# A decoder layer on one core: the matmuls that turn the 1/rms of queries and keys come later in the program, and one output-gate pair moves ahead of the convolutions

## The chip, the core and the metric

The kernel runs on one core of a Trainium2 chip. The metric is device time in microseconds (us), lower is better. Before the change three runs took 2025.02, 2026.25 and 2028.8 us, with a median of 2026.25 us.

## The reference, cut to what matters

One layer of a hybrid decoder, SEQ = 1024 tokens of D_MODEL = 1024, float32 throughout:

```python
x = x + 0.5*(1+gate0) * swiglu1(rmsnorm(x)*(1+scale0)+shift0)
u = (rmsnorm(x)*(1+scale1)+shift1) @ w_in       # in-projection
x = x + (1+gate1) * concat(diff_attention(...), mlstm(...)) @ w_out
x = x + 0.5*(1+gate2) * swiglu2(rmsnorm(x)*(1+scale2)+shift2)

# differential attention: 4 heads, two 64-wide queries and keys each
q = rmsnorm(q.reshape(..., 4, 2, 64), g_q); k = rmsnorm(k.reshape(..., 4, 2, 64), g_k)
q = partial_rope(q, cos, sin);              k = partial_rope(k, cos, sin)
# mLSTM: q and k go through a causal convolution of 4 taps and silu;
# its result h is gated:  sigmoid(o_pre) * h
```

The change touches the in-projection alone: the rms of queries and keys, the values and the output gate of the mLSTM, and the convolutions.

## The kernel before, in words

The layer runs in stages one behind the other: the first feed-forward block to about 715 us, the in-projection to about 1085, the heads (attention and mLSTM, interleaved) to about 1276, the out-projection to about 1390, the second feed-forward block to the end.

**A product.** The in-projection is made of calls of `wino` (L240), each giving a 256x1024 piece of u, transposed, by a Winograd scheme on halves: seven products of 512x128 by 512x512, each of 12 matmuls, since every operand is split into a high and a low part and three of the four cross products are kept (`mm3`, L199 to L201). In a call the products come in the order B11, T2, T1, B21, T3, B22, T4. Their weights come by DMA on SyncE's queue (`wraw`), are summed (`wsum`, L194, `sf`), rounded by ScalarE (`split_w`, L187, `whi`) and subtracted by VectorE (L188, `wlo`). VectorE combines the products into the four quarters of the result (L229): "11" is what B11 and B21 add up to and is handed out by `got11`, "22" and "12" come after T3 and B22, "21" after T4.

**The calls around the change.** Four calls `wqk[0..3]` give queries (0, 1) and keys (2, 3), then `wmv[1]` gives the second half of the mLSTM's values, `wcv[0..3]` what the four convolutions need, and `wmo[0]`, `wmo[1]` the output gates. Then the heads begin.

**The rms of queries and keys.** Each quarter of a query or key is squared by ScalarE and added up by VectorE (`k`, L582 to L587). When both calls of the queries are through, `qk_finish` (L591) is put into the list `pending`, which the next `wino` runs behind its product T1 (`late`). It sums the squares over each 64 rows by eight small matmuls (L598; the profile shows two records for each such float32 matmul), takes the reciprocal root on VectorE by ten short instructions (L601, then `rsqrt`, L349 to L354), and for each half of the tokens copies the result sixteenfold (ScalarE, L605, tile `c`), turns it by four matmuls against the identity (L609) and copies it out of PSUM (ScalarE, L611). `qk_turned` (L614) multiplies queries or keys by it, applies the rotary part, rounds (L628, `qhi`), takes the rest (L629) and writes both to memory (`qkd`, L631) on SyncE's queue.

**Values, convolutions and gates.** A quarter of the values is turned by four transposes (L642, into `modps`), copied by ScalarE (L644, `vt`) and stored. These turns too wait in `pending` for the next call. `got11` of a convolution copies its quarter into `cu` (ScalarE, L746); L735 to L739 are the taps, silu and the store to `mlqk`, 512 KB each. `got11` of an output gate is a tanh (ScalarE, L756, tile `vc`) followed by a multiply and a store to `mlo`, 256 KB each. The tiles `cu` lie where the tiles `qraw` of queries and keys lay (`pq.close()` gives up the one pool and the next takes its space).

**What sets the order.** The program's text is not the order: a scheduler that simulates a time line sets the order of instructions on each engine, subject to dependencies and priorities (`split_w` has a raised one). `keep_in_program_order` holds an instruction behind the one traced before it on its engine. Each engine then runs its own list strictly in that order.

Of the kernel before, what the change touches and what calls it, by code (L numbers as in the profile page):

```python
# [25 lines left out]
P = 128  # L26
# [107 lines left out]
class Layer:  # L134
    def __init__(self, tc, A, es):
        self.tc, self.nc, self.A, self.es = tc, tc.nc, A, es
        nc = self.nc
        pool = lambda name, **k: es.enter_context(tc.tile_pool(name=name, **k))
        self.const = pool("const", bufs=1)
        c = self.const  # L140
        self.ones = c.tile([P, 1], F32, name="ones")
        nc.vector.memset(self.ones, 1.0)
        self.eps = c.tile([P, 1], F32, name="eps")
        nc.vector.memset(self.eps, EPS)
        self.mod = c.tile([P, 72], F32, name="mod")
        self.G = c.tile([P, 24], F32, name="G")
        self.gate = c.tile([P, 24], F32, name="gate")
        self.bada = c.tile([P, 72], F32, name="bada")
        self.gn = c.tile([P, 24], F32, name="gn")
        self.cs = c.tile([P, KT], F32, name="cs")  # L150
        self.B, self.full = {}, {}
        self.nct = 3
        self.sums = nc.gpsimd
        self.pending = []

    def ps(self):
        return self.mmps.tile([P, HT], F32, tag="mm", name="mm")
# [4 lines left out]
    def late(self):  # L162

        p, self.pending = self.pending, []
        for f in p:
            f()

# [58 lines left out]
    def wino(self, src, got11, out, got, st=None):  # L226

        nc = self.nc
        add = lambda o, a, b: nc.vector.tensor_tensor(out=o, in0=a, in1=b, op=ALU.add)  # L229
        t = lambda n: self.tmp.tile([P, HT], F32, tag=n, name=n)  # L230
        r1, r2 = self.load_raw(src[0]), self.load_raw(src[1])
        a11, a21, a12, a22 = r1[:, 0], r1[:, 1], r2[:, 0], r2[:, 1]
        if st is None:
            x = self.ps()
            self.prod(x, self.split_w(a11), "B11", True)
            p1 = t("p1")
            nc.scalar.copy(out=p1, in_=x)
            s1 = self.wsum(a21, a22, ALU.add)
            s2 = self.wsum(s1, a11, ALU.subtract)
            y6, z5 = self.ps(), self.ps()  # L240
            self.prod(y6, self.split_w(s2), "T2", True)
            u2 = t("u2")
            add(u2, p1, y6)
            self.prod(z5, self.split_w(s1), "T1", True)
            self.late()
            w = t("w")
            add(w, u2, z5)
            self.prod(x, self.split_w(a12), "B21", False)
            got11(x)
            y7, z3 = self.ps(), self.ps()  # L250
            self.prod(y7, self.split_w(self.wsum(a11, a21, ALU.subtract)), "T3", True)
            c22 = out("22")
            add(c22, w, y7)
            self.prod(z3, self.split_w(self.wsum(a12, s2, ALU.subtract)), "B22", True)
        else:
            p1 = st["p1"]
            s1 = self.wsum(a21, a22, ALU.add)
            s2 = self.wsum(s1, a11, ALU.subtract)
            z3, z5, y7, y6 = (self.ps() for _ in range(4))
            self.prod(z3, self.split_w(self.wsum(a12, s2, ALU.subtract)), "B22", True)  # L260
            self.prod(z5, self.split_w(s1), "T1", True)
            self.late()
            self.prod(y7, self.split_w(self.wsum(a11, a21, ALU.subtract)), "T3", True)
            self.prod(y6, self.split_w(s2), "T2", True)
            u2 = t("u2")
            add(u2, p1, y6)
            w = t("w")
            add(w, u2, z5)
            c22 = out("22")
            add(c22, w, y7)  # L270
        got("22", c22)
        c12 = out("12")
        add(c12, w, z3)
        got("12", c12)
        self.prod(y7, self.split_w(a22), "T4", False)
        c21 = out("21")
        add(c21, u2, y7)
        got("21", c21)
# [312 lines left out]
    def qk_finish(self, which):  # L591

        nc = self.nc
        ps = self.ps()
        for hf in range(2):
            for i in range(4):
                c = 8 * (4 * hf + i)
                nc.tensor.matmul(ps[:, c:c + 8], self.accs[which][hf][:, i * P:(i + 1) * P], self.bd[:, 0:P:16],  # L598
                                 start=True, stop=True, skip_group_check=True)
        v, y, t = (self.qkp.tile([P, 64], F32, tag=f"qn{i}", name=f"qn{i}") for i in range(3))  # L600
        nc.vector.tensor_scalar(out=v, in0=ps[:, 0:64], scalar1=1.0 / 64, scalar2=EPS, op0=ALU.mult, op1=ALU.add)  # L601
        self.rsqrt(y, t, v)
        for hf in range(2):
            r = self.ct()
            nc.scalar.copy(out=r.rearrange("p (c d) -> p c d", d=16),  # L605
                           in_=y[:, 32 * hf:32 * hf + 32].unsqueeze(2).broadcast_to([P, 32, 16]))
            ps = self.ps()
            for i in range(4):
                nc.tensor.matmul(ps[:, i * P:(i + 1) * P], r[:, i * P:(i + 1) * P], self.ident,  # L609
                                 start=True, stop=True, skip_group_check=True)  # L610
            nc.scalar.copy(out=r, in_=ps)  # L611
            self.qk_turned(which, hf, r)

    def qk_turned(self, which, hf, r):  # L614
        nc = self.nc
# [359 lines left out]
def build(tc, yT, **A):  # L975
    nc = tc.nc
    with ExitStack() as es:
        L = Layer(tc, A, es)
# [40 lines left out]
        rs = []  # L1019
# [122 lines left out]
        def mlv_store(pr):  # L1142
            def store(e, hf, v):
                nc.sync.dma_start(out=L.mlv[2 * pr + e][:, 4 * hf:4 * hf + 4, :], in_=v)
            return store
# [37 lines left out]
        L.rst = load_const(L.gp, "rst", [P, T])  # L1183
        L.wino(A["wdv"][0], *dvh[0], starts[0])
        late, L.pending = L.pending, []
        L.gate_rows(graw)
        turn, L.pending = L.pending, late
# [23 lines left out]
        for which in range(2):  # L1211
            for tp in range(2):
                i = 2 * which + tp
                seen, out, got = L.qk_handlers(which, tp)
# [8 lines left out]
                    L.wino(A["wqk"][i], seen11, out, got)  # L1223
            L.pending.append(lambda w=which: L.qk_finish(w))
        L.wino(A["wmv"][1], *L.v_handlers(mlv_store(1)))
        pq.close()

        pq, qpool = stack("right")
        L.cvp = qpool("cvp", bufs=2)
        for h in range(4):  # L1230
            L.wino(A["wcv"][h], *L.conv_handlers(h))
        for pr in range(2):
            L.wino(A["wmo"][pr], *L.o_handlers(pr))
        pq.close()
        pm.close()
        pt.close()
# [132 lines left out]
```

## Time and profile before

| | |
|---|---|
| median of three runs | 2026.25 us (2025.02 to 2028.8) |
| profiled execution | 2028.85 us, its span 2027.1 us |
| mean granted clock of TensorE | 0.976 of full speed |
| TensorE busy | 1924.4 us, 95% of the span |
| VectorE, ScalarE, GpSimd busy | 73%, 38%, 14% |
| TensorE's longest waits, 860 to 1110 us | 9.7 (L883), 9.1 in four (L609), 3.4 (L642) |

PE is TensorE, ACT ScalarE, DVE VectorE, POOL GpSimd and SP SyncE. An idle time stands in brackets behind an instruction, with what released it. PEclk is the clock granted to TensorE as a share of 2.4 GHz; 0.50 is its lower level, 1.2 GHz, and a value between is a stretch in which it changed. Times are us from the start of the span.

### The profile page before, as it was taken

To read this page: it belongs to the slowest core of one execution; us is meant where nothing else is said; L and a number is where in the kernel's file an instruction comes from. 1 tells how busy PE (TensorE), PEld (TensorE's weight loads), DVE (VectorE), ACT (ScalarE), POOL (GpSimd) and SP (SyncE) were. 2 spreads that over 40 slices of the span, in tenths; PEclk is the share of its full clock that TensorE was granted. 3 is DMA by queue.
4 is the path that set the end of the run, shared out by engine and by line. 5 is a ranking of instruction groups with operands and counts; after the bars stand their busy time and mean duration, and the time that the engine had idled before them with its cause. 6 is when DMAs were issued, how large, how long until landed. Compare 5 with 4: busy or idle time off the path is not lost.

```text
span 2027.1 us, 24590 instructions
## 1 busy us (share of the span) xinstructions
PE 1924.4 (95%) x8870; PEld 1588.1 (78%) x8870; DVE 1476.6 (73%) x2609; ACT 774.1 (38%) x1494; POOL 292.3 (14%) x249
## 2 busy tenths in 40 slices
PE   4999999999999988989997999988999999999999
PEld 3778888888888876777786877876888888888887
DVE  8998888777766679577794987479766555556665
ACT  4522232222232356334443876255222233222232
POOL 0111212211121100000002211004212111121120
PEclk9999999999999989988998999999999999999999
DMA  8344333223221242223427963121111111111113
GB/s 303 125 146 140 115 118 106 85 82 104 101 72 58 94 146 71 79 97 129 150 111 203 185 131 120 53 83 63 63 63 42 63 63 42 49 56 53 53 63 125
DMA packets 86794, 202.82 MB, mean 100 GB/s; under 512 B 10128, under 2 KB 18704, under 8 KB 86672
## 3 DMA queue, kind: packets, MB, share of 16 engines
q1 hardware_dynamic: 77504, 184.93, 26.6%
q0 software_dynamic: 7840, 14.75, 4.1%
q8 instruction: 70, 1.15, 0.2%
q10 hardware_dynamic: 1328, 1.57, 0.2%
q14 instruction: 52, 0.43, 0.1%
HBM read 174.02 MB, written 27.26 MB: 99 GB/s over the span
## 4 chain that ended last, share of the span: by engine, by line
PE 83%; DVE 8%; ACT 4%; DMA 3%; issue 1%; POOL 1%; SPq 0%; DVEq 0%; ACTq 0%; POOLq 0%
PE mm L199 25%; PE mm L200 25%; PE mm L201 25%; PE t L820 1%; DVE adaacc L324 1%; DVE S L378 1%; DVE wlo L188 1%; DMA qkd<-qhi 1%; PE s L793 1%; ACT S L380 1%; POOL sf L194 1%; DVE S L429 1%; DMA adac<-in_wada 1%; PE s L794 1%; PE t L816 0%
## 5 line engine op out<-in xcount | busy, mean ns | idle before, releaser
L187 ACT CAST whi<-wraw 128x512 fp32r<-128x512 f32 x308 | 190.9, 621 | 481.8 <-PE mm L200 454.6
L199 PE MATMUL mm<-S,whi 128*128 128x512 f32 x900 | 354.5, 395 | 7.4 <-ACT whi L187 3.1
L200 PE MATMUL mm<-S,whi 128*128 128x512 f32 x900 | 353.7, 393 | 0.0
L201 PE MATMUL mm<-S,wlo 128*128 128x512 f32 x900 | 352.8, 393 | 0.0
L529 DVE SCALAR_TENSOR_TENSOR x<-mm,gate,x 128x512 f32<-128x512 f32 x368 | 269.5, 745 | 95.1 <-PE mm L201 93.9
L187 ACT CAST whi<-sf 128x512 fp32r<-128x512 f32 x224 | 138.8, 621 | 414.9 <-PE mm L200 387.3
L188 DVE TENSOR_TENSOR wlo<-wraw,whi 128x512 fp32r<-128x512 f32 x300 | 210.4, 702 | 89.5 <-ACT whi L187 77.5
L200 PE MATMUL mm<-glo,whi 128*128 128x512 f32 x672 | 262.5, 391 | 0.0
L201 PE MATMUL mm<-ghi,wlo 128*128 128x512 f32 x672 | 261.6, 392 | 0.0
L199 PE MATMUL mm<-ghi,whi 128*128 128x512 f32 x672 | 260.8, 393 | 0.1
L194 POOL TENSOR_TENSOR sf<-wraw 128x512 f32<-128x512 f32 x84 | 120.9, 1439 | 597.4 <-DMA wraw<-in_w 380.6
L199 PEld LDWEIGHTS mm<-S,whi 128*128 128x128 f32 x900 | 171.2, 190 | 44.2 <-ACT whi L187 3.5
L201 PEld LDWEIGHTS mm<-S,wlo 128*128 128x128 f32 x900 | 170.8, 190 | 36.5 <-DVE wlo L188 0.8
L200 PEld LDWEIGHTS mm<-S,whi 128*128 128x128 f32 x900 | 170.9, 190 | 35.3
L188 DVE TENSOR_TENSOR wlo<-sf,whi 128x512 fp32r<-128x512 f32 x224 | 156.1, 697 | 38.4 <-ACT whi L187 38.0
L199 PEld LDWEIGHTS mm<-ghi,whi 128*128 128x128 f32 x672 | 126.8, 189 | 26.4 <-ACT ghi L522 0.6
L200 PEld LDWEIGHTS mm<-glo,whi 128*128 128x128 f32 x672 | 126.9, 189 | 26.2
L201 PEld LDWEIGHTS mm<-ghi,wlo 128*128 128x128 f32 x672 | 126.8, 189 | 26.3
L229 DVE TENSOR_TENSOR c<-w,mm 128x512 f32<-128x512 f32 x84 | 57.2, 686 | 99.5 <-PE mm L201 99.4
L194 POOL TENSOR_TENSOR sf<-wraw,sf 128x512 f32<-128x512 f32 x42 | 64.1, 1526 | 444.8 <-DVE wlo L188 356.0
L324 DVE SCALAR_TENSOR_TENSOR adaacc<-adac,cs,adaacc 128x256 f32<-128x256 f32 x196 | 110.0, 561 | 10.7 <-DMA adac<-in_wada 9.3
L199 PE MATMUL mm<-B11h,whi 128*128 128x512 f32 x248 | 99.6, 409 | 11.4 <-ACT B11h L383 7.2
(332 smaller groups left out, 3418.1 us busy)
## 6 DMA issues: line engine op xcount, KB each, us to landing
wraw<-in_w SPq DMA_DIRECT2D x142, 512.0 KB
adac<-in_wada SPq DMA_DIRECT2D x112, 256.0 KB
ok<-qkd POOLq DMA_DIRECT2D x32, 256.0 KB, 8.0
adaraw<-in_wada SPq DMA_DIRECT2D x12, 512.0 KB
wraw<-in_wo SPq DMA_DIRECT2D x12, 512.0 KB
x<-in_xT SPq DMA_DIRECT2D x16, 256.0 KB
xd<-x SPq DMA_DIRECT2D x16, 256.0 KB
wraw<-in_wqk SPq DMA_DIRECT2D x8, 512.0 KB
```

The source lines that it names most:

```text
L187: nc.scalar.copy(out=hi, in_=raw)
L188: (eng or nc.vector).tensor_tensor(out=lo, in0=raw, in1=hi.bitcast(F32), op=ALU.subtract)
L194: self.sums.tensor_tensor(out=s, in0=a, in1=b, op=op)
L199: nc.tensor.matmul(ps, whi, xhi, start=first, stop=False, skip_group_check=True)
L200: nc.tensor.matmul(ps, whi, xlo, start=False, stop=False, skip_group_check=True)
L201: nc.tensor.matmul(ps, wlo, xhi, start=False, stop=last, skip_group_check=True)
L229: add = lambda o, a, b: nc.vector.tensor_tensor(out=o, in0=a, in1=b, op=ALU.add)
L324: nc.vector.scalar_tensor_tensor(out=acc, in0=raws[k], scalar=self.cs[:, k:k + 1], in1=acc, op0=ALU.mult, op1=ALU.add)
L378: eng.tensor_tensor(out=h, in0=x, in1=r, op=ALU.mult)
L380: self.nc.scalar.activation(out=h, in_=h, func=AF.Identity, scale=self.G[:, g:g + 1], bias=self.mod[:, s:s + 1])
L429: e.tensor_tensor(out=T[n][1], in0=v, in1=T[n][0].bitcast(F32), op=ALU.subtract)
L529: self.nc.vector.scalar_tensor_tensor(out=x, in0=ps, scalar=self.gate[:, g:g + 1], in1=x, op0=ALU.mult, op1=ALU.add)
```

## The change

`qk_finish` now makes both sixteenfold copies first and puts the rest (turn, copy out, `qk_turned`) into a second list, `next`. A new `later()` runs that list right behind the product B21 of the call. The turning matmuls are held in program order. In the sequence of calls `wmo[0]` now stands right behind `wmv[1]`, ahead of the change of pools and of the convolutions; `wmo[1]` stays behind them. Line numbers of the changed kernel are 6 or 7 higher up to its sums (L605), then 13 or 14.

```diff
     def late(self):
 
         p, self.pending = self.pending, []
         for f in p:
             f()
 
+    def later(self):
+
+        p, self.next = self.next, []
+        for f in p:
+            f()
...
             self.prod(x, self.split_w(a12), "B21", False)
+            self.later()
             got11(x)
...
+        rs = []
         for hf in range(2):
             r = self.ct()
             nc.scalar.copy(out=r.rearrange("p (c d) -> p c d", d=16),
                            in_=y[:, 32 * hf:32 * hf + 32].unsqueeze(2).broadcast_to([P, 32, 16]))
-            ps = self.ps()
-            for i in range(4):
-                nc.tensor.matmul(ps[:, i * P:(i + 1) * P], r[:, i * P:(i + 1) * P], self.ident,
-                                 start=True, stop=True, skip_group_check=True)
-            nc.scalar.copy(out=r, in_=ps)
-            self.qk_turned(which, hf, r)
+            rs.append(r)
+
+        def turn():
+            for hf, r in enumerate(rs):
+                ps = self.ps()
+                for i in range(4):
+                    self.tc.keep_in_program_order(
+                        nc.tensor.matmul(ps[:, i * P:(i + 1) * P], r[:, i * P:(i + 1) * P], self.ident,
+                                         start=True, stop=True, skip_group_check=True))
+                nc.scalar.copy(out=r, in_=ps)
+                self.qk_turned(which, hf, r)
+        self.next.append(turn)
...
         L.wino(A["wmv"][1], *L.v_handlers(mlv_store(1)))
+        L.wino(A["wmo"][0], *L.o_handlers(0))
         pq.close()
...
         for h in range(4):
             L.wino(A["wcv"][h], *L.conv_handlers(h))
-        for pr in range(2):
-            L.wino(A["wmo"][pr], *L.o_handlers(pr))
+        L.wino(A["wmo"][1], *L.o_handlers(1))
         pq.close()
```

**ScalarE at the turn of the queries.** `c` is the sixteenfold copy, `qn` the reciprocal root. Before:

```order
L605 COPY c_7729<-qn1_7716 128x512
L611 COPY c_7729<-mm_7731 128x512
L605 COPY c_7766<-qn1_7716 128x512
L611 COPY c_7766<-mm_7768 128x512
L187 CAST whi_7922<-sf_7918 128x512
```

and now:

```order
L613 COPY c_7729<-qn1_7716 128x512
L613 COPY c_7731<-qn1_7716 128x512
L624 COPY c_7729<-mm_7751 128x512
L624 COPY c_7731<-mm_7786 128x512
L193 CAST whi_7922<-sf_7918 128x512
```

Both copies now stand ahead of both copies out of PSUM. On TensorE nothing moved at this place: in either kernel the eight turning matmuls follow the eight of the sums directly, and the product B21 of the call stands ahead of the sums.

**TensorE at the sums of the keys.** `mm_8111` are the sums, `modps` the turn of a value quarter, `mm_8052` is product B21 of the call `wmv[1]`, `mm_7979` product T4 of the last call of the keys. Before:

```order
L199 MATMUL mm_8052<-B21h3_205,whi_8210 128x512
L200 MATMUL mm_8052<-B21l3_206,whi_8210 128x512
L201 MATMUL mm_8052<-B21h3_205,wlo_8211 128x512
L598 MATMUL mm_8111<-bd_7335,k_7823 128x8 x4
L598 MATMUL mm_8111<-bd_7335,k_7865 128x8 x4
L642 MATMUL modps_8359<-ident_225,vc_8226 128x128 x4
L609 MATMUL mm_8136<-ident_225,c_8134 128x128 x4
L609 MATMUL mm_8173<-ident_225,c_8171 128x128 x4
L199 MATMUL mm_8228<-S50_6634,whi_8232 128x512
```

and now:

```order
L205 MATMUL mm_7979<-S43_6733,whi_8027 128x512
L206 MATMUL mm_7979<-S33_6735,whi_8027 128x512
L207 MATMUL mm_7979<-S43_6733,wlo_8028 128x512
L656 MATMUL modps_8351<-ident_225,vc_8226 128x128 x4
L605 MATMUL mm_8111<-bd_7335,k_7823 128x8 x4
L605 MATMUL mm_8111<-bd_7335,k_7865 128x8 x4
L622 MATMUL mm_8156<-ident_225,c_8134 128x128 x4
L622 MATMUL mm_8191<-ident_225,c_8136 128x128 x4
L205 MATMUL mm_8228<-S50_6634,whi_8232 128x512
```

The value transposes moved from behind the sums to ahead of them, and T4 of the keys, between which and the sums 28 matmuls stood before, now stands right ahead of the transposes and the sums. T4 gives the last quarter of the keys, whose squares go into `k_7823` and `k_7865`.

**ScalarE in the call behind the values.** `vt` are value quarters out of `modps`, `cu` the first quarter of convolution 0, `vc_8401` that of output gate 0. A name ending in `_49` in brackets is a semaphore: of an engine, or of a DMA queue slot (DMAHW). Before:

```order
L644 COPY vt_8372<-modps_8367 128x512 [waits PE_49]
L187 CAST whi_8490<-wraw_8485 128x512 [waits DMAHW1_49,PE_49]
L746 COPY cu_8292<-mm_8300 128x512 [waits DMAHW3_49,DMAHW7_49,DVE_49,PE_49]
L644 COPY vt_8380<-modps_8375 128x512 [waits PE_49]
L187 CAST whi_8514<-sf_8510 128x512 [waits DVE_49,PE_49,Activation_49]
L187 CAST whi_8532<-sf_8508 128x512 [waits PE_49,Activation_49]
L735 ACTIVATE cv_8450<-cu_8292,convb_6794,convw_6792 128x1024 [waits DVE_49,DMAHW1_49,Activation_49,Pool_49]
```

and now:

```order
L658 COPY vt_8364<-modps_8359 128x512 [waits PE_49]
L642 CAST qhi_8215<-qraw_8022 128x512 [waits DMAHW1_49,DVE_49]
L193 CAST whi_8487<-wraw_8482 128x512 [waits PE_49]
L770 ACTIVATE vc_8401<-mm_8292 128x512 [waits PE_49]
L642 CAST qhi_8221<-qraw_7999 128x512 [waits DMAHW3_49,DVE_49]
L193 CAST whi_8511<-sf_8507 128x512 [waits DVE_49,PE_49]
L658 COPY vt_8372<-modps_8367 128x512 [waits DMAHW2_49,PE_49]
L193 CAST whi_8529<-sf_8505 128x512 [waits PE_49]
L770 ACTIVATE vc_8425<-vc_8425 128x512 [waits DVE_49]
L658 COPY vt_8380<-modps_8375 128x512 [waits DMAHW6_49,PE_49,Activation_49]
L770 ACTIVATE vc_8448<-vc_8448 128x512 [waits DVE_49]
```

Where the copy into `cu` stood, which waits for DMAs, there is now the tanh of the output gate, which waits for TensorE alone. The copy into `cu` stands one call later:

```order
L770 ACTIVATE vc_8469<-vc_8469 128x512 [waits DVE_49]
L193 CAST whi_8611<-wraw_8484 128x512 [waits PE_49,Activation_49]
L193 CAST whi_8644<-wraw_8639 128x512 [waits DMAHW3_49,PE_49,Activation_49]
L760 COPY cu_8478<-mm_8486 128x512 [waits DMAHW7_49,DMAHW0_49,PE_49]
L193 CAST whi_8668<-sf_8664 128x512 [waits DVE_49,PE_49,Activation_49]
```

The last copy `vt_8380` now has a wait on a DMA slot that it had not. GpSimd's list is the same in both kernels. The list of ScalarE has seven loads of an activation table before and after. In the heads, some 110 of about 1,070 rows of TensorE's list stand in other places.

## Rows read from the trace of the kernel before

**Rows 1.** The page, busy time of TensorE, its share of the span and instructions.

```profile
PE 1924.4 (95%) x8870; PEld 1588.1 (78%) x8870; DVE 1476.6 (73%) x2609; ACT 774.1 (38%) x1494; POOL 292.3 (14%) x249
```

**Rows 2.** TensorE's waits from 860 to 1110: line, releaser, us in all, times, longest.

```profile
PE mm L883 <- DMA mq<-mlqk: 9.7, 1, 9.7
PE mm L609 <- ACT c L605: 9.1, 4, 3.5
```

**Rows 3.** TensorE's timeline, queries: start, us, instruction, idle before and releaser.

```profile
889.73 1.95 PE L598 MATMUL mm<-bd,k 128*128 128x8 f32 x16 [0.76 <-DVE k L587]
895.21 2.08 PE L609 MATMUL mm<-ident,c 128*128 128x128 f32 x8 [3.53 <-ACT c L605]
898.53 2.08 PE L609 MATMUL mm<-ident,c 128*128 128x128 f32 x8 [1.25 <-ACT c L605]
900.27 0.77 PE L199 MATMUL mm<-S,whi 128*128 128x512 f32 x1
```

**Rows 4.** Busy time in windows, queries: us, engines, then granted clock (PEclk), DMA.

```profile
894.00:895.00 1.00, 0.00 (x0) 0.00 (x0) 0.45 (x2) 0.46 (x1) 0.00 (x0) 0.60 0.12 49
...
904.00:905.00 1.00, 1.00 (x5) 0.82 (x4) 1.00 (x3) 0.00 (x0) 0.00 (x0) 0.78 0.00 0
...
907.00:920.00 13.00, 13.00 (x59) 10.76 (x58) 9.59 (x17) 5.23 (x11) 0.00 (x0) 1.00 0.48 167
```

**Rows 5.** TensorE's timeline, keys.

```profile
941.12 1.85 PE L598 MATMUL mm<-bd,k 128*128 128x8 f32 x16
942.82 0.64 PE L642 MATMUL modps<-ident,vc 128*128 128x128 f32 x4
946.49 2.08 PE L609 MATMUL mm<-ident,c 128*128 128x128 f32 x8 [3.04 <-ACT c L605]
949.82 2.08 PE L609 MATMUL mm<-ident,c 128*128 128x128 f32 x8 [1.25 <-ACT c L605]
```

**Rows 6.** Busy time in windows, keys.

```profile
945.00:946.00 1.00, 0.00 (x0) 0.00 (x0) 0.69 (x4) 0.17 (x1) 0.00 (x0) 0.70 0.86 311
...
955.00:956.00 1.00, 1.00 (x4) 0.76 (x4) 1.00 (x3) 0.00 (x0) 0.00 (x0) 0.68 0.00 0
```

**Rows 7.** VectorE's timeline after the query turn, and a group of ScalarE's lines.

```profile
916.72 0.69 DVE L229 TENSOR_TENSOR qraw<-w,mm 128x512 f32<-128x512 f32 x1 [3.30 <-DMA qkd<-qraw]
...
923.21 0.69 DVE L587 TENSOR_TENSOR k<-k,c 128x512 f32<-128x512 f32 x1
...
L586 ACT ACTIVATE c<-qraw 128x512 f32<-128x512 f32 x12 | 7.4, 630 | 3.0 <-DVE qraw L229 2.9
```

**Rows 8.** The stop at 984: chain, ScalarE's timeline, TensorE's timeline, windows.

```profile
976.03 7.04 DMA qkd<-qraw
...
970.40 0.62 ACT L628 CAST qhi<-qraw 128x512 fp32r<-128x512 f32 x1 [4.19 <-DMA qkd<-qhi]
...
983.23 0.59 ACT L746 COPY cu<-mm 128x512 f32<-128x512 f32 x1 [8.87 <-DMA qkd<-qraw]
...
984.36 1.11 PE L642 MATMUL modps<-ident,vc 128*128 128x128 f32 x4 [3.37 <-ACT vt L644]
...
983.00:989.00 6.00, 4.64 (x13) 3.87 (x14) 3.99 (x6) 3.82 (x6) 0.33 (x4) 0.50 0.44 168
989.00:990.00 1.00, 1.00 (x4) 0.76 (x4) 1.00 (x2) 0.00 (x0) 0.00 (x0) 0.61 0.58 219
```

**Rows 9.** Opening of the heads: ScalarE's queue, TensorE, and the window 1085 to 1097.

```profile
1084.85 0.44 ACTq L863 DMA_DIRECT2D mq<-mlqk  x1
1088.72 0.59 ACTq L864 DMA_DIRECT2D mv<-mlv  x1
...
1094.67 2.04 PE L883 MATMUL mm<-mq,mk 128*128 128x128 f32 x8 [9.68 <-DMA mq<-mlqk]
...
1085.00:1097.00 12.00, 2.33 (x11) 2.36 (x12) 0.72 (x4) 2.50 (x6) 0.00 (x0) 0.66 1.12 370
```

**Rows 10.** TensorE's waits from 1106 to 1290, the longest row.

```profile
PE s L793 <- ACT e L799: 4.7, 7, 1.3
```

More of the change, by code (lines that the diff above doesn't have):

```diff
@@ L153, in __init__ @@
         self.sums = nc.gpsimd
-        self.pending = []
+        self.pending, self.next = [], []
     def ps(self):
```

## The prediction

> **What bounds the kernel now.** I read the busy shares first, then TensorE's waits, then its timeline at each wait, with the granted clock beside it. TensorE is busy 95% of the span [rows 1], so the end moves by what TensorE idles and by what it does at half rate, and by little else. In the stretch that the change touches, its waits are few and long: one of 9.7 us for the first head's queries, then four of 9.1 us together for the copies that the turn needs [rows 2], and one of 3.4 us for a copy `vt` [rows 8]. Each is followed by a stretch at 0.50 of the clock. That is the second price of a stop, and often the larger one.
>
> **Queries.** The reader is to see one stop in two pieces: 3.53 us from the sums' end to the first turn, then 2.08 us of turning, then 1.25 us more, because the second copy waits behind the copy out of PSUM [rows 3]. With both copies made first the 1.25 us goes: a pass of ScalarE over a tile of this size takes 0.63 us [rows 7], so the second copy ends that much behind the first, and the first half's turn of 2.08 us covers it. The first 3.53 us stays, since the order shows nothing between sums and turn: the product that the new place was to put between them stood ahead of the sums already.
>
> The clock: the window at 894 is a mean of 0.60, so it fell at about 894.2; that at 904 is 0.78, so it rose at about 904.4 [rows 4]. From the first turn at 895.21 that is 9.2 us, 8.0 of them work at half rate. How much work at half rate comes after a stop with no second pause is read at the third stop: there work resumes at 984.36 and the clock is back at about 989.8 (0.61 in the last window), 5.4 us [rows 8]. If the queries take that course, (8.0 - 5.4) / 2 = 1.3 us is saved beside the 1.25: 2.5 us. Against it: VectorE waits at 916.72 for 3.30 us for a write of the queries to land [rows 7], and what hangs on that write comes no earlier for a second turn that ends earlier, since the first copy out of PSUM is at its old time. In the new order the weights' low parts stand ahead of that waiting addition, which loosens it. I take 1.8 of the 2.5; the ends are 2.5 and 0.
>
> **Keys.** The same 1.25 us goes. But T4 of the keys now stands last. Its path to the sums is an addition (0.69), then the square (0.63) beside a split and an addition that stand ahead of the last sum on VectorE (2 x 0.69, so these decide), then that sum (0.69) [rows 7]: about 2.8 us, of which the value transposes cover 0.64 [rows 5]. So TensorE stops for 2.1 us ahead of the sums, where it did not stop. Behind them nothing covers the chain any more: from the sums' end, 941.12 + 1.85 = 942.97, to the turn at 946.49 it is 3.52 us, of which 3.04 was idle. Sum of the idle: 2.1 + 3.52 - 3.04 - 1.25 = 1.3 us more. On the clock, half rate lasted from about 945.4 to 955.6 [rows 6], 7.9 us of work from 946.49; by the 5.4 of the third stop 1.25 us would be saved. With an extra stop ahead, the clock may also fall before the sums; I count half, 0.6. Keys: 0.7 us lost. Ends: 0.6 gained (the two other VectorE instructions do not stand in the way, so 0.6 more idle, and the clock gives all), 2.2 lost (the clock gives nothing, and the sums of 1.85 run at half rate).
>
> **The stop at 984.** ScalarE sits 8.87 us in front of the copy `cu`, until a write of the keys has landed: 976.03 plus 7.04 [rows 8]. `vt` stands behind it, and TensorE waits 3.37 us for that. From 984.36 to 989.8 it works at half rate, 5.4 us, which costs 2.7. Together 6.1 us. In the new order a tanh stands there that waits for TensorE alone, and `cu` comes one call later. A call is 84 matmuls; 59 take 13.0 us at the full clock [rows 4], so 18.5 us. The copy was due at 974.36 (983.23 - 8.87) and will be at about 993, 10 us behind the landing at 983.07: that is the cover. What becomes late next is `vt_8380`, which now waits for the store of an earlier `vt`; that store stands where the cast at 970.40 stood [rows 8], and with the 7.04 of the last write it lands at about 978, an estimate, when TensorE is at the product B22 of the call and needs nothing of that copy. I take 6.1 gained; the other end is 0.
>
> The tanh earlier than silu costs no table load on ScalarE (seven before and now).
>
> **The opening of the heads.** The first head's queries are loaded from 1084.85 and TensorE stands until 1094.67 [rows 9]; the window moved 370 GB/s. The order of these loads is as before, each behind the last tanh. But convolution 3 is now one call nearer to the heads: its second store, 512 KB, comes about when the second output gates' first tanh does, and not a call earlier. At 370 GB/s, 512 KB is 1.4 us; both its stores are 2.8. I take 0.7 lost, with ends 0 and 2.8. The value load shows that such a load can be held: it left only at 1088.72.
>
> The Trainium skill says in DMA: Bandwidth & Descriptors, Issuing engines are not separate DMA queues, that DMAs of all issuing engines run on the same 16 engines and interleave. The trace agrees in this window: its DMA share is 1.12 with loads from two queues and stores from a third. By that rule the moved store lengthens the loads by its full share, and the sum below would be 0.7 us less gain; were queues separate it would be 0.7 us more.
>
> **The heads.** Some tenth of TensorE's list there stands elsewhere. The waits in that stretch are short, at most 1.3 us, 4.7 in the largest group [rows 10]. I take 0, with 3 us to either side (about two such waits made or removed).
>
> **Sum.** -1.8 (queries) + 0.7 (keys) - 6.1 (stop at 984) + 0.7 (opening) + 0 = -6.5 us. The profiled execution took 2028.85 us with a span of 2027.1, so 2022.3 for it (the 1.75 us around the span stay). It stands 2.6 us above the median of the three runs; on the median, 2026.25 - 6.5 = 2019.8 us, rounded.
>
> **Rivals.**
>
> 1. *The turn gains nothing.* The title's point, a product between sums and turn, does not come about. If also the query chain is bound by the landing write, queries are 0, and keys 2.2 lost. For it: the 3.30 us wait [rows 7]. Against: two 1.25 us pauses that the new order removes visibly. Time: 0 + 2.2 - 6.1 + 0.7 = -3.2, 2023.0 us. Chance 0.20.
>
> 2. *The wait of 984 comes back a few instructions on.* ScalarE stops at `vt_8380` because the store before it lands late, behind the writes. It decides from a landing after about 982, 4 us later than reckoned, and holds the roundings of the next call's weights, which TensorE needs. For it: the new wait in the order, and 7 us per write. Against: it was issued earlier than the last write of the keys. Then the 6.1 is not gained: -1.8 + 0.7 + 0.7 = -0.4, 2025.8 us. Chance 0.13.
>
> 3. *Slower: the heads lose in their new order.* A tile that was ready is now late there, once or several times, because the interleaving of attention and mLSTM was drawn up anew. It decides from 6.5 us, where it eats all that is gained. The nearest rows: 9.7 us for the first head's queries [rows 2] and 4.7 for the softmax [rows 10]. A second wait of the size of the first gives -6.5 + 9.7 = +3.2, 2029.4 us. For it: the waits there are numerous. Against: none exceeds 1.3 us, and the work is the same. Chance 0.12.
>
> **How the numbers follow.** The forecast has a chance of 0.55, with a range of its own from 2016 to 2023. Low end of all: the best values, -2.5 - 0.6 - 6.1 + 0 - 3 = -12.2, 2014; this I keep. High end: rival 1 and rival 2 lie inside 2027.5, rival 3 is mostly left out. Range 2014 to 2027.5. A measurement of this kernel tells about 0.2% from no change, 4.05 us, so faster means below 2022.2. The forecast lies below that in some 0.85 of its cases (0.47), rival 1 in 0.45 of them (0.09), rival 2 in 0.15 (0.02): faster 0.58. Slower, above 2030.3: of rival 3 about half (0.06), and 0.04 for the tails of the others: 0.10. The rest, 0.32, is no change.
>
> **What would show it.** Right: ScalarE's copies `c` stand side by side in the profile, and the two turns run on without a pause; TensorE idles about 2 us between T4 of the keys and their sums; no wait of TensorE for `vt` at 984, with the clock at full there; `cu` of convolution 0 waits for no DMA; the first head's queries are waited for some 10 to 11 us. Wrong: a new wait for a DMA on ScalarE between 975 and 985, a longer stop ahead of the heads, or waits in the heads that sum to more than 12 us.

## The result: slower, and the profile after

| | before | after |
|---|---|---|
| median, runs beside each other | 2027.53 us (4) | 2037.49 us (4) |
| ratio, 95% interval | | 1.0064 (1.0049 to 1.008) |
| profiled execution, span | 2028.85, 2027.1 us | 2040.72, 2038.9 us |
| mean granted clock | 0.976 | 0.977 |

The change costs 13 us by the ratio (10 to 16) and 10 us by the two medians, where 6.5 were to be gained. TensorE does the same work in the same busy time, so [rows 1] has hardly a new digit; the page alone would show nothing:

```profile
PE 1924.6 (94%) x8870; PEld 1586.2 (78%) x8870; DVE 1471.0 (72%) x2609; ACT 775.0 (38%) x1494; POOL 290.6 (14%) x249
```

TensorE's waits in the stretch of the change (line, releaser, us in all, times, longest), which answer to [rows 2], do show it:

```profile
PE mm L897 <- DMA mq<-mlqk: 10.5, 1, 10.5
PE mm L207 <- DVE wlo L194: 9.9, 3, 5.0
PE mm L622 <- ACT c L613: 7.1, 2, 3.6
PE mm L605 <- DVE k L594: 2.9, 2, 2.1
```

The turns wait 7.1 us in two stops instead of 9.1 in four. The 3.4 us for `vt` are gone. New is the second row: 9.9 us for low parts of weights, a wait that the profile of before does not have and the prediction does not name.

**The two new stops.** TensorE's timeline at both, then the granted clock in windows behind them (the last but two column of each row):

```profile
930.46 0.39 PE L205 MATMUL mm<-B21h,whi 128*128 128x512 f32 x1
...
936.08 0.79 PE L207 MATMUL mm<-B21h,wlo 128*128 128x512 f32 x1 [5.00 <-DVE wlo L194]
...
997.39 0.79 PE L207 MATMUL mm<-B21h,wlo 128*128 128x512 f32 x1 [4.58 <-DVE wlo L194]
```

```profile
936.00:940.00 4.00, 3.92 (x9) 3.13 (x10) 4.00 (x8) 1.77 (x3) 0.00 (x0) 0.50 0.00 0
940.00:942.00 2.00, 2.00 (x7) 1.55 (x6) 1.97 (x4) 1.10 (x2) 0.00 (x0) 0.69 0.00 0
...
997.00:1002.00 5.00, 4.61 (x11) 3.64 (x12) 5.00 (x10) 1.46 (x3) 0.32 (x4) 0.50 0.16 60
1002.00:1004.00 2.00, 2.00 (x9) 1.58 (x8) 1.14 (x2) 0.78 (x2) 0.00 (x0) 0.83 0.36 114
```

Each stop stands in the middle of a product B21, at its third matmul, the first that needs a low part. Behind each the clock is at 0.50: for 5.1 us of work at the first (to about 941.2), for 5.3 at the second (to about 1002.7), which costs half of that again. So the stops cost 5.0 + 2.6 = 7.6 and 4.6 + 2.6 = 7.2 us.

Who makes `wlo` late is read on VectorE. Its timeline at either stop:

```profile
934.73 0.69 DVE L200 TENSOR_TENSOR sf<-wraw 128x512 f32<-128x512 f32 x1 [7.36 <-DMA wraw<-in_wmo]
935.34 0.68 DVE L194 TENSOR_TENSOR wlo<-wraw,whi 128x512 fp32r<-128x512 f32 x1
...
996.04 0.69 DVE L200 TENSOR_TENSOR sf<-wraw 128x512 f32<-128x512 f32 x1 [10.94 <-DMA wraw<-in_wcv]
996.65 0.68 DVE L194 TENSOR_TENSOR wlo<-wraw,whi 128x512 fp32r<-128x512 f32 x1
```

VectorE is held 7.36 us by a sum `sf` of two weight blocks of the next call, one of which has not landed. The subtraction that B21 needs stands right behind it, and its own operands are long there. In before the same two instructions stand in the same order, and TensorE does not wait for them. Its VectorE, its TensorE at the same B21, and SyncE's queue:

```profile
933.42 0.68 DVE L587 TENSOR_TENSOR k<-k,c 128x512 f32<-128x512 f32 x1
934.41 0.69 DVE L194 TENSOR_TENSOR sf<-wraw 128x512 f32<-128x512 f32 x1 [0.30 <-DVE k L587]
935.02 0.69 DVE L188 TENSOR_TENSOR wlo<-wraw,whi 128x512 fp32r<-128x512 f32 x1
...
938.40 0.39 PE L199 MATMUL mm<-B21h,whi 128*128 128x512 f32 x1
...
938.85 0.39 PE L201 MATMUL mm<-B21h,wlo 128*128 128x512 f32 x1
...
926.48 1.19 SPq L178 DMA_DIRECT2D wraw<-in_wcv  x1
...
927.76 1.06 SPq L178 DMA_DIRECT2D wraw<-in_wcv  x1
```

and SyncE's queue after:

```profile
924.48 1.04 SPq L184 DMA_DIRECT2D wraw<-in_wmo  x1
925.61 1.44 SPq L645 DMA_DIRECT2D qkd<-qraw  x1
927.14 0.61 SPq L184 DMA_DIRECT2D wraw<-in_wmo  x1
```

Counted from the sums of the queries (889.73 before, 886.42 after), since these are the last common point:

- B21 begins 48.67 us on in before and 44.04 in after, 4.6 earlier. 2.7 of it is T4 of the keys, whose 12 matmuls stood ahead of B21 and now stand behind it.
- The second of the two loads leaves 38.03 us on in before and 40.72 in after, 2.7 later. Half of that the first load has too (36.75 and 38.06); the rest is a write of the queries that now stands between the two.
- The load also takes longer: 7.51 us after. In before the sum that needs it starts 6.65 us after it left (934.41 - 927.76), so it took no longer than that there: 0.9 us more, at the least.

Before, the low part was ready at 935.71 and needed at 938.85: 3.1 us of slack. 4.6 + 2.7 + 0.9 = 8.2 us take that away and leave 5.1 us, the stop of 5.0. The chain of waits after (start, us, what) names this load, and another for the second stop:

```profile
927.14 7.51 DMA wraw<-in_wmo
...
987.14 8.78 DMA wraw<-in_wcv
```

The second stop repeats the first one call on: the load of convolution 0 that `sf` waits for leaves 40.8 us behind the sums of the keys (987.14 - 946.37), behind their writes. Where the keys' copies are not first (e2_gate_only, below), the two such loads leave together from 979.39 on, 37.1 us behind the sums of its keys (at 942.29), and nothing waits.

**What answers to the other rows.** TensorE at the queries and keys [rows 3, 5], and windows behind the two turns [rows 4, 6]:

```profile
886.42 1.95 PE L605 MATMUL mm<-bd,k 128*128 128x8 f32 x16 [0.76 <-DVE k L594]
891.90 3.78 PE L622 MATMUL mm<-ident,c 128*128 128x128 f32 x16 [3.53 <-ACT c L613]
...
946.37 1.85 PE L605 MATMUL mm<-bd,k 128*128 128x8 f32 x15 [2.14 <-DVE k L594]
...
952.01 3.41 PE L622 MATMUL mm<-ident,c 128*128 128x128 f32 x16 [3.58 <-ACT c L613]
```

```profile
896.00:897.00 1.00, 1.00 (x4) 0.81 (x3) 1.00 (x3) 0.36 (x1) 0.00 (x0) 0.57 0.00 0
...
952.00:955.00 3.00, 2.99 (x14) 2.99 (x15) 0.20 (x1) 1.06 (x2) 0.00 (x0) 0.52 0.00 0
955.00:956.00 1.00, 1.00 (x8) 0.87 (x8) 1.00 (x2) 0.49 (x1) 0.00 (x0) 1.00 0.00 0
```

Both turns run in one piece, and the clock is back sooner: after 4.9 us of work at half rate at the queries (8.0 before), after some 2.9 at the keys (7.9 before). ScalarE at the old place of `cu` and at its new one [rows 8], then TensorE at the opening of the heads [rows 9], and its longest wait in the heads [rows 10]:

```profile
978.37 0.59 ACT L770 ACTIVATE vc<-mm 128x512 f32<-128x512 f32 x1
...
1002.20 0.58 ACT L760 COPY cu<-mm 128x512 f32<-128x512 f32 x1
```

```profile
1098.58 2.04 PE L897 MATMUL mm<-mq,mk 128*128 128x128 f32 x8 [10.51 <-DMA mq<-mlqk]
```

```profile
PE s L807 <- ACT e L813: 5.6, 8, 1.7
```

`cu` waits for nothing. The first product of the heads waits 0.83 us longer than it did. From there the heads take 233.0 us (from that product to the last matmul of the first group of the out-projection) where before took 225.0: idle time in it rose from 11.4 to 15.4 us, and the same 1349 instructions of TensorE were busy 217.7 instead of 213.7.

**The account**, after against before, from the sums of the queries on: queries -1.25 of pause and (8.0 - 4.9) / 2 = 1.55 of clock, -2.8; keys +2.14 ahead of the sums, then 3.58 instead of 4.29 idle and (7.9 - 2.9) / 2 = 2.5 less of clock, -1.1; `vt` -6.1; opening +0.8; first stop +7.6; second stop +7.2; heads +8.0; two waits of 0.77 and 0.30 for VectorE on the way +1.1. That is +14.7; the profiles give +15.2. The sums of the queries began 3.3 us earlier in this one execution of after, on the same order of TensorE, in which the clock returned sooner after a stop at 717; so the spans differ by 11.9.

### The profile page after: what moved, and what is told of

It is laid out like the page before. It is cut to its first block, busy times and chain, and to the rows that moved or that the text cites. A ratio compares the mean times of both kernels' runs of the same rounds, so it can differ in the third digit from the quotient of the medians.

```text
span 2038.9 us, 24592 instructions
## 1 busy us (share of the span) xinstructions
PE 1924.6 (94%) x8870; PEld 1586.2 (78%) x8870; DVE 1471.0 (72%) x2609; ACT 775.0 (38%) x1494; POOL 290.6 (14%) x249
## 4 chain that ended last, share of the span: by engine, by line
PE 80%; DVE 9%; DMA 6%; ACT 3%; issue 1%; POOL 1%; SPq 0%; DVEq 0%; ACTq 0%; POOLq 0%
PE mm L205 25%; PE mm L207 25%; PE mm L206 25%; PE t L834 1%; DMA qkd<-qhi 1%; DVE S L385 1%; DMA adac<-in_wada 1%; DMA wraw<-in_w 1%; DVE nm L811 1%; DVE wlo L194 1%; DMA mv<-mlv 1%; PE s L807 1%; POOL sf L200 1%; DVE S L427 1%; DVE adaacc L331 1%
## 5 line engine op out<-in xcount | busy, mean ns | idle before, releaser
L235 DVE TENSOR_TENSOR c<-w,mm 128x512 f32<-128x512 f32 x84 | 57.2, 686 | 98.7 <-PE mm L207 98.6
L205 PE MATMUL mm<-B11h,whi 128*128 128x512 f32 x248 | 99.9, 409 | 10.7 <-ACT B11h L390 7.2
```

Of the source, the lines that this page charges most:

```text
L205: nc.tensor.matmul(ps, whi, xhi, start=first, stop=False, skip_group_check=True)
```

## Experiments

All ratios are against the kernel before, measured beside it. The profile of each is divided at four points: the sums of the queries, the sums of the keys, the first product of the heads (L883 of before), the last matmul of the first group of the out-projection. The two heads' orders are called X (that of before) and Y (that of after); TensorE's rows there are the same in all runs of one letter, but for the last three, which share one more order, near Y. The last column gives TensorE's waits for `wlo` behind the late sum; the last three have waits at other places. Against the times that were expected, the medians of e2, e5, e6 and e7 lie inside and that of e3 at the lower edge; those of e1, e4, e8, e9, e10 and e11 are above.

| kernel | ratio (95%) | to keys' sums | to heads | heads | stop 1, 2 |
|---|---|---|---|---|---|
| before | 1 | 51.4 | 153.6 | 225.0 X | none |
| after | 1.0064 (1.0049, 1.008) | 60.0 | 152.2 | 233.0 Y | 5.0, 4.6 |
| e1_turn_only | 1.0081 (1.0068, 1.0095) | 60.4 | 154.7 | 231.8 Y | 5.2, 7.9 |
| e2_gate_only | 0.9983 (0.9973, 0.9993) | 51.3 | 148.0 | 227.2 X | none |
| e3_pool_sums | 1.0014 (1.0003, 1.0025) | 53.5 | 151.9 | 227.1 X | 0, 2.3 |
| e4_act_loads | 1.003 (1.0018, 1.0042) | 57.2 | 148.1 | 231.7 Y | 1.3, 0 |
| e5_gate_q | 1.0014 (1.0002, 1.0026) | 60.5 | 147.1 | 223.8 X | 4.7, 0 |
| e6_gate_k | 1.0014 (1.0001, 1.0027) | 51.8 | 148.6 | 231.0 Y | 0, 2.4 |
| e7_copies_only | 1.0082 (1.0064, 1.01) | 59.9 | 152.1 | 233.1 Y | 5.5, 6.0 |
| e8_pool_act | 1.0016 (1.0003, 1.0029) | 57.5 | 147.6 | 224.2 X | 0, 0 |
| e9_t3_pool | 1.0047 (1.0033, 1.0061) | 56.8 | 151.7 | 234.1 | other |
| e10_t3_pool_act | 1.0031 (1.0018, 1.0043) | 53.5 | 147.3 | 233.5 | other |
| e11_t3 | 1.0037 (1.0023, 1.0051) | 56.5 | 152.2 | 233.5 | other |

**Each half of the change alone.** e1_turn_only is the change without the moved call; e2_gate_only is before with this alone:

```diff
         L.wino(A["wmv"][1], *L.v_handlers(mlv_store(1)))
+        L.wino(A["wmo"][0], *L.o_handlers(0))
         pq.close()
...
-        for pr in range(2):
-            L.wino(A["wmo"][pr], *L.o_handlers(pr))
+        L.wino(A["wmo"][1], *L.o_handlers(1))
```

> The turn's part of the change alone (the output-gate pair back behind the convolutions). Theory 1 (late weights): VectorE stands at the first weights sum of the next call, whose load left SyncE late behind the writes of the queries, and the low part wlo that TensorE needs stands behind it; the turn's part alone moved that sum ahead. Then the stop of about 5 us in product B21 of wmv[1] is here too, and the stop at `cu` comes back: 2033 to 2040 us. Theory 2 (the gate pair: its stores, and the new order in the heads, cost it): no stop in B21, about 2 us gained at the queries: 2023 to 2028 us.

> The output-gate pair moved, the turn as before. Theory 1: no stop in B21 of wmv[1]; TensorE's wait of 3.4 us for `vt` and its half-rate stretch are gone: 2020 to 2025 us, unless the weights of the call after next come late as well (then up to 2028). Theory 2: the second stop of about 5 us on wlo and the lost 8 us in the heads are here: 2031 to 2038 us.

The turn's part alone has both stops and the heads' order Y. It reads slower than the whole change, though the two intervals overlap. ScalarE's wait at `cu` is back in it (12.3 us at 1001.5), but TensorE's stop there is for `wlo`. The moved call alone is faster by 3.4 us (1.4 to 5.5), has no wait for `vt` and no new one, and keeps the heads' order. Its stretch to the heads is 5.6 us shorter, where the stop at 984 was reckoned at 6.1. It is the fastest of all kernels here. TensorE's waits in it are the opening of the heads and the old turns:

```profile
PE mm L883 <- DMA mq<-mlqk: 10.2, 1, 10.2
PE mm L609 <- ACT c L605: 9.1, 4, 3.5
```

**The wait of VectorE, taken away in two ways.** e3_pool_sums has the weights of the moved call summed by GpSimd, so that VectorE has no `sf` to be held by. e4_act_loads leaves the sums where they are and issues the loads of that call and of the first two convolutions from ScalarE's queue, past the writes on SyncE's.

```diff
+        L.sums = nc.gpsimd
         L.wino(A["wmo"][0], *L.o_handlers(0))
+        L.sums = nc.vector
```

```diff
-        self.nc.sync.dma_start(out=raw, in_=src)
+        self.wq.dma_start(out=raw, in_=src)
...
+        L.wq = nc.scalar
         L.wino(A["wmo"][0], *L.o_handlers(0))
...
             L.wino(A["wcv"][h], *L.conv_handlers(h))
+            if h == 1:
+                L.wq = nc.sync
```

> The changed kernel with the four weights sums of wmo[0] on GpSimd in place of VectorE; nothing else. Theory 1: VectorE no longer stands at that sum, so the 5.0 us stop in B21 of wmv[1] and its half-rate stretch go; the second stop (weights of wcv[1]) stays: 2029 to 2034 us. If the weights are needed by TensorE itself at that time, the stop only moves one product on: 2036 to 2039. Theory 2: no gain, 2036 to 2039 us.

> The changed kernel with the weight loads of wmo[0], wcv[0] and wcv[1] issued on ScalarE's queue, so that they do not stand behind the writes on SyncE's. Theory 1 in its form that the place in SyncE's list makes the loads late: both stops on wlo (5.0 and 4.6 us) go or fall under 1.5 us each: 2024 to 2030 us. Rival: the loads leave earlier but share the DMA engines with the writes and land no earlier: both stops stay within 1.5 us of their size, 2034 to 2039 us.

In e3 the first stop is gone: GpSimd is held instead, and TensorE passes the third matmul of B21 without a wait. Its GpSimd and its TensorE:

```profile
939.03 1.29 POOL L200 TENSOR_TENSOR sf<-wraw 128x512 f32<-128x512 f32 x1 [176.83 <-DMA wraw<-in_wmo]
...
934.92 0.39 PE L207 MATMUL mm<-B21h,wlo 128*128 128x512 f32 x1
```

The sum begins at 939.03, 4 us after B21 needed its low part, and nobody misses it. So the sum was in B21's way and not in its chain. The gain of e3 over after is not the price of this stop alone, since its heads are back at order X. In e4 the load leaves 927.16 - 889.18 = 37.98 us behind the sums of the queries, 2.7 earlier than in after, and the stop shrinks from 5.0 to 1.3, with a new one of 1.8 us, for an addition into `qraw`, ahead of it. The load itself cannot leave much earlier: its buffer is given back by a subtraction of VectorE that ends at 925.4. Chain of e4:

```profile
924.75 0.61 DVE wlo L194
925.37 1.64 ACTq L184
...
927.16 8.67 DMA wraw<-in_wmo
```

It takes 8.67 us there against 7.51 in after. The Trainium skill says in DMA: Bandwidth & Descriptors, Issuing engines are not separate DMA queues, that DMAs run on the same 16 engines whichever engine started them. This trace does not settle it: the load that left past the writes took longer beside them, but one on SyncE's own queue took 8.78 us in after. e4 stays 0.3% slower than before: 5.8 us more to the sums of the keys, 5.5 less from there to the heads, and 6.7 more in the heads, which keep order Y. With one stop gone and the other cut, the heads' price stands; it is one of its own. Nor is it a matter of reaching them late: e5 (below) reaches them at 1096.08 us and takes 223.8, e6 at 1089.27 and takes 231.0.

**Which of the copies does it.** e7_copies_only is before with nothing but the two copies made first, no second list, no matmuls held in program order (the pin), no moved call. e5_gate_q and e6_gate_k are e2 with the copies first for the queries alone, or the keys alone.

```diff
+        rs = []
         for hf in range(2):
             r = self.ct()
             nc.scalar.copy(out=r.rearrange("p (c d) -> p c d", d=16),
                            in_=y[:, 32 * hf:32 * hf + 32].unsqueeze(2).broadcast_to([P, 32, 16]))
+            rs.append(r)
+        for hf, r in enumerate(rs):
             ps = self.ps()
```

e5 and e6 make the first loop depend on the call, here e5:

```diff
+        rs = [self.ct(), self.ct()] if which == 0 else None
...
+        if rs:
+            for hf, r in enumerate(rs):
+                spread(hf, r)
```

> The kernel before with both sixteenfold copies made ahead of the turn, for queries and keys; no deferral, no pin, no output-gate move. Theory 1: the order on TensorE and VectorE is that of the turn's part alone, so the time is too: 2040 to 2047 us, with the stop of 5 us in B21. Rival (the place behind B21 and the pin matter): within 3 us of the kernel before, 2024 to 2030 us.

> The output-gate pair moved, and both sixteenfold copies made before the turn for the queries alone; nothing deferred or pinned. The order has the weights sum ahead of wlo on VectorE and T4 of the keys last, but the heads stand as in the kernel before. Theory 1 (two separate losses: VectorE at the late weights, and the order of the heads): the stop of 5 us in B21 of wmv[1] is here, queries' sums to keys' sums about 60 us (51 before), the heads take 225 to 228 us: 2029 to 2034 us. Rival (the deferral behind B21 and its pin do the harm): no stop, 2021 to 2025 us.

> The output-gate pair moved, and both copies first for the keys alone. The order up to the keys' sums is that of the kernel before, the heads stand as in the changed kernel. Theory 1: no stop in B21, queries' sums to keys' sums 51 to 52 us, but the heads take 231 to 233 us from the first head's q k product to the last of the out-projection's first group, against 225 to 227: 2025 to 2030 us. Rival (the heads lose only because what comes before them is late): heads at 225 to 228, 2020 to 2024 us.

e7 loses what e1 loses (1.0082 and 1.0081), and TensorE's and VectorE's order is that of e1 row for row. So the second list behind B21 and the pin change nothing: two copies side by side are the whole of that part. The queries' copies bring the first stop (e5: TensorE 938.35, then the sums of the keys with their 2.15), the keys' copies bring the second stop and order Y (e6), and each makes e2 slower by about 0.3%, 6 us. Together that is 0.6%, where after stands 0.8% above e2; the intervals do not tell these apart. The second stop is smaller in e6 than in after (2.4 against 4.6) and stands in another product. TensorE of e5, then of e6, then VectorE of e7, which is held by the same kind of sum as in after, here of the first convolution's weights:

```profile
938.35 0.79 PE L201 MATMUL mm<-B21h,wlo 128*128 128x512 f32 x1 [4.70 <-DVE wlo L188]
949.00 1.95 PE L598 MATMUL mm<-bd,k 128*128 128x8 f32 x16 [2.15 <-DVE k L587]
```

```profile
993.66 0.50 PE L201 MATMUL mm<-S,wlo 128*128 128x512 f32 x1 [2.44 <-DVE wlo L188]
```

```profile
936.62 0.69 DVE L194 TENSOR_TENSOR sf<-wraw 128x512 f32<-128x512 f32 x1 [6.99 <-DMA wraw<-in_wcv]
```

**Both remedies together.** e8_pool_act is e3 and e4 in one.

> The changed kernel with the weights sums of wmo[0] on GpSimd and the weight loads of wmo[0], wcv[0] and wcv[1] on ScalarE's queue together. The heads stand as in the kernel before. Theory 1: neither the stop of 5.0 nor that of 4.6 us, heads 225 to 228 us: 2021 to 2027 us. Rival (the stops only move on to the next instruction that needs the weights): 2029 us or more, as with the sums alone.

This missed. Both stops are gone and the heads have order X, but it is not faster than before. The stretch to the sums of the keys is 57.5 us instead of 51.4. TensorE waits twice for VectorE's additions into `qraw`. The first wait, for a tile that a write of the queries holds, is there in after too (0.77 us); the second, of 2.58 us, is new, and the clock is at half rate behind it (0.54 in the window 928 to 931). TensorE, then ScalarE, VectorE and TensorE at the second:

```profile
919.43 0.50 PE L205 MATMUL mm<-S,whi 128*128 128x512 f32 x1 [0.89 <-DVE qraw L235]
...
921.31 4.29 ACTq L184 DMA_DIRECT2D wraw<-in_wmo  x1
925.65 0.63 ACT L593 ACTIVATE c<-qraw 128x512 f32<-128x512 f32 x1 [3.96 <-issue]
...
926.31 0.69 DVE L594 TENSOR_TENSOR k<-k,c 128x512 f32<-128x512 f32 x1 [3.16 <-ACT c L593]
...
928.35 0.77 PE L205 MATMUL mm<-S,whi 128*128 128x512 f32 x1 [2.58 <-DVE qraw L235]
```

The remedy makes this wait itself. ScalarE stands 4.29 us at the issue of a moved load: until 923.16 for its buffer, which a subtraction of VectorE gives back, then 2.44 us more. The square of a keys' quarter (`c`) stands behind it on ScalarE, VectorE waits 3.16 us for that square, and the addition that TensorE needs stands behind this wait. In e4 it is the same: an issue of 3.49 us at 923.51, VectorE held for 2.36, TensorE for 1.78. The stop is turned into another of its own kind, on another engine.

**The title taken at its word.** In after no product stands between sums and turn. e11_t3 puts the second list behind product T3 of the call, one product later, so that one does; e9_t3_pool adds GpSimd's sums of e3, e10_t3_pool_act also the loads of e4.

```diff
-            self.later()
             got11(x)
...
             self.prod(y7, self.split_w(self.wsum(a11, a21, ALU.subtract)), "T3", True)
+            self.later()
```

> The changed kernel with the turn behind product T3 of the call in place of B21, so that a product really stands between sums and turn, and the weights sums of wmo[0] on GpSimd. Theory 1: TensorE's waits for the copies `c` fall from 3.5 to about 0.8 us each (T3 covers 2.7) and the clock stays at its upper level over them, which is worth some 10 us beside the run with GpSimd's sums alone (2029); the heads stand nearly as in the changed kernel and cost 4 to 6 of it: 2020 to 2026 us. Rival (the turned queries come later, and VectorE and the writes behind them hold TensorE elsewhere): 2028 us or more.

> The same with the weight loads of wmo[0], wcv[0] and wcv[1] on ScalarE's queue. Theory 1: the second stop on wlo, of the weights of wcv[1], goes too: 1 to 4 us less than with SyncE's queue, 2018 to 2024 us. Rival (the earlier loads take the DMA engines from the writes of the queries, and TensorE waits for VectorE's additions that wait for these): the same or up to 3 us more.

> The turn behind product T3 alone; the weights sums on VectorE and all loads on SyncE's queue, as in the changed kernel. Theory 1: on VectorE the low part wlo of B21 stands ahead of the late weights sum in this order, so the stop in B21 does not come, or only as one on the next low part: 2022 to 2030 us. Rival (the sum holds VectorE in any order): 2032 us or more.

The turn's wait does fall, from 3.53 to 0.67 us, and the time gets no better than 0.3% above before. TensorE of e9, from the turn of the queries on, then ScalarE at the last of these waits:

```profile
895.26 2.05 PE L622 MATMUL mm<-ident,c 128*128 128x128 f32 x16 [0.67 <-ACT c L613]
918.95 0.50 PE L205 MATMUL mm<-S,whi 128*128 128x512 f32 x1 [2.56 <-DVE qraw L235]
930.68 0.80 PE L205 MATMUL mm<-S,whi 128*128 128x512 f32 x1 [6.00 <-ACT qraw L1235]
...
930.04 0.59 ACT L1235 COPY qraw<-mm 128x512 f32<-128x512 f32 x1 [5.39 <-DMA qkd<-qraw]
```

What was won at 895 is lost at 918 and 930. The turn comes later by a product's time, the writes of the queries with it, and the tiles that the keys' quarters are to be put into are those that these writes hold: ScalarE stands 5.39 us for one. So the turn's own wait is not what bounds this stretch. Each beside the run from which it differs by the place of the turn alone: e11 is less slow than after (1.0037 against 1.0064, the intervals just overlap), and e9 is slower than e3 (1.0047 against 1.0014).

## Why the prediction was wrong, point by point

**The step that failed** is the one on the keys: "But T4 of the keys now stands last." It priced only that T4 comes later (2.1 us ahead of the sums; measured 2.14). The other side of the same move is that B21 comes earlier, by T4's 2.7 us and by what the queries had won, 4.6 us in all, and B21 needs a low part that stands on VectorE behind a sum that waits for a load, which lands later (2.7 and 0.9 us). The fence on the keys showed B21 of the values, `wlo_8211` and all, ahead of the sums; the prediction does not ask what `wlo_8211` stands behind on VectorE, nor when the load under that leaves SyncE, and so no term and no rival held it. Its price is 7.6 us, and 7.2 for the same pattern at the load of convolution 0: 14.8 us together, nearly as much as the whole loss of 15.2 in the profiles.

**The heads.** "Some tenth of TensorE's list there stands elsewhere", taken as 0 with 3 to either side; measured +8.0 in this profile, +3.8 in e6 against e2 with the same change of order. Rival 3 had the mechanism and priced it by one long wait; there is none. Idle time rose by 4.0, to 15.4, in many short waits (the prediction's sign of being wrong was 12), the longest of 2.3 for a load of values, where before had one of 2.2 at the same step; and the busy time of the same instructions by 4.0, of which two profiles of one order also show 2.2 (213.7 before, 215.9 in e2). Over all profiles of orders X and Y the heads take 223.8 to 227.2 and 231.0 to 233.1, so the order is worth 4 to 9 us. Why the scheduler draws up Y when the keys' copies are made first stays open, and no run tells it.

**What was right.** Queries: -2.8 against -1.8 (the 1.25 went, the clock gave 1.55 where 1.3 was reckoned, and the late write cost the 1.1 of two small waits, close to the discount). The stop at 984: 6.1 gained in the account, 5.6 in e2; the cover of `cu` held, and rival 2, a new wait at `vt_8380`, did not come. Keys, apart from the failed step: 1.1 gained where 0.7 lost was forecast. The idle ahead of the sums is 2.14 for 2.1; the clock gave 2.5 instead of 0.6, since its spell at half rate began before the turn and was mostly spent idle (0.51 at 948 to 950), which is luck: the prediction does not have it. Opening: +0.83 for +0.7; this wait is 10.1 to 10.7 us in all runs with the moved call and 9.7 to 10.0 in the three without it. So the terms that were priced sum to -2.8 + 1.1 - 1.1 - 6.1 + 0.8 = -8.1 us, a little better than forecast; all that made the kernel slower lay in terms set at nothing.

**Rival 1** was right that no product came between sums and turn, but the pauses of 1.25 us went all the same. With a product there (e9 to e11) the kernel is still not faster than before.

## What to carry to other kernels

A move in a scheduled program must be followed on every engine, and to both sides: what now comes later, and what thereby comes earlier, with the operand it needs and what stands ahead of that operand's producer. On an engine that runs its list in order, an instruction that waits for a load holds all behind it, so for each such instruction the slack is to be read beforehand: landing of its load against the time at which the next thing behind it is needed (3.1 us here). Two changes in one should be timed apart; here the half worth keeping was hidden by the other.

## What the runs showed of the hardware

A load of 512 KB took 7.5 to 8.8 us where it left among writes of 256 KB (927.14 and 987.14 after, 927.16 in e4), and at most 6.65 at the same place in before. ScalarE, where a load was issued from its queue before the buffer was free, stood at the issue for 4.29 us (e8) and 3.49 us (e4), with its next activation behind it. And the work at half rate behind a stop was not of one length: 4.9 to 5.3 us of work at three of them after, but 2.9 at the keys, where the clock had fallen at about 948 and the work resumed at 952, and 7.9 and 8.0 in before, where a second pause of 1.25 us lay in it.
